# Memory tokens loaded channels first, their weights in packed blocks, and the opening of a four-branch encoder kernel put in another order

## The chip, the cores and the metric

The kernel runs on one NeuronCore of a Trainium2 chip. The metric is the device time of one execution in microseconds, 968.35 us at the median of three runs of the kernel before. The engines are named as the profile names them: PE (TensorE, matmuls), PEld (its weight loads), DVE (VectorE), ACT (ScalarE), POOL (GpSimd), SP (SyncE, which issues most DMAs). Each engine works through its own queue in order and waits on semaphores.

## What is computed

One layer of an encoder, batch 1, 1024 tokens of width 1024, all in float32. Only the parts that the change touches are shown; the four branches of the mixer (`mlstm_chunkwise`, `multiscale_pool`, `rwkv7_time_mix`, `forgetting_attention`) stand between them.

```python
def rms_norm(x, g):
    x32 = x.astype(jnp.float32)
    y = x32 * lax.rsqrt(jnp.mean(x32 * x32, axis=-1, keepdims=True) + NORM_EPS)
    return (y * g).astype(x.dtype)
...
    mem_n = rms_norm(mem, mem_norm_g)             # 256 memory tokens
    h = rms_norm(x, pre_norm_g[l])
    proj = h @ w_in[l] + b_in[l]                  # 1024 x 3728, feeds the four branches
    ...
    x = x + rms_norm(y @ w_out[l], post_norm_g[l])
    hm = rms_norm(x, xattn_pre_g[l])
    # memory attention: k, v = split(mem_n @ wkv), o = softmax(q k / 16) v, o @ wo
    x = x + rms_norm(memory_cross_attention(hm, mem_n, xattn_wq[l], xattn_wkv[l], xattn_wo[l]), xattn_post_g[l])
```

## The kernel before

All products are split in two halves, as `a = hi + lo`: `mm3` (lines 136 to 139) issues three matmuls (hi·hi, hi·lo, lo·hi) into one PSUM group. The hi half is a copy in a rounded type made by ACT, the lo half a subtraction.

The program opens with the **memory stage**, the part that changes. In the order of PE:

1. 16 transposes (line 215) of the two 128 x 1024 tiles of `mem` give `mT` (channels in the partitions), which ACT (line 163) and DVE (line 164) split while they multiply by `mem_norm_g`.
2. Eight blocks `cp` (the loop behind line 259) make `mem @ wkv`, 256 columns each: 8 channel groups x 2 column halves x 3 matmuls of 256 columns, 48 matmuls. The result is multiplied by the memory tokens' inverse norms `RS` (line 268). Blocks 0 to 3 are K and go to DRAM (`kTd`, line 270), 4 to 7 are V and stay as `KV`.
3. In between, after block `cp`, the 128-token tile `cp - 1` of `x` is transposed (`xtile`, line 252: 8 transposes of 128 x 128, in two PSUM tiles of four) and split (lines 160, 161) into `h` and `l`. `xnorm` (lines 240 to 245) has loaded and normalised it: Square with a row sum on ACT (149), a power on POOL (143, 144), and one DVE instruction that multiplies by the inverse norm and by `pre_norm_g` (151). Tiles 6 and 7 are both transposed behind block 7.
4. `vwrow` (line 325 on) multiplies V by `xattn_wo`, four heads of 24 matmuls with 512 columns, copied by ACT (335) and stored to `vwd` (336).

Then the input projection `h @ w_in` starts, and with it the rest of the program (lines 345 on), which the change does not touch.

Weights come in **pieces** of 128 x 512 floats (256 KB) through `wload` (lines 110 to 127): SP issues the load into one of four `wr` buffers (two of `wp1`, two of `wp0`), ACT casts to `wh` (line 122), and the lo half `wl` is made on DVE (line 124) for every second piece and on POOL (line 126) for the others, while `wp0` is open:

```python
            SC.copy(hi, raw)
            if cur["wp0"] is not None and wcount["wr"] % 2:
                V.tensor_tensor(lo, raw, f32(hi), op=ALU.subtract)
            else:
                G.tensor_tensor(lo, raw, f32(hi), op=ALU.subtract)
```

A block of step 2 takes four pieces, and a head of step 4 takes four. A `wr` buffer is free again when its lo half is made; `wh` and `wl` have eight buffers each, free when PE is done with them. A scheduler orders each engine's queue by priority, weight loads ahead of other work; the built program's order is shown below where the change moves it.

Of the kernel before, what the change touches and what calls it, by code (L numbers as in the profile page):

```python
# [36 lines left out]
def tile_trunk(ctx: ExitStack, tc: tile.TileContext, a, out, dbg=None):  # L37
# [143 lines left out]
    xp = Pool("xp", {"x": 2, "xn": 3, "gbc": 1})  # L181
# [20 lines left out]
    V.memset(mhalf, -0.5)  # L202


    mss = m0.one("mss", [128, 2])
    mTh = [m0("mT", [128, 4, 256], F32R) for _ in range(2)]
    mTl = [m0("mT", [128, 4, 256], F32R) for _ in range(2)]
    for kp in range(4):
        if kp == 1:
            tc.cur_priority = pr0  # L210
        p = ps("tr", [128, 2, 256])
        for i in range(2):
            for kk in range(2):
                k = 2 * kp + kk
                T.transpose(p[:, kk, i * 128:(i + 1) * 128], mx_[i][:, k * 128:(k + 1) * 128], ident)
        for kk in range(2):
            q, r = divmod(2 * kp + kk, 4)
            split_evac(mTh[q][:, r, :], mTl[q][:, r, :], p[:, kk, :], mg[:, 2 * kp + kk:2 * kp + kk + 1])
    for i in range(2):
        SC.activation(xp("xn", [128, 1024]), mx_[i], AF.Square, accum_out=mss[:, i:i + 1])  # L220
    mr = rstd_pow("tn", mss, D, EPS, 2)
    rE = m0.one("rE", [128, 2, 128])
    V.tensor_copy(rE, mr[:, :, None].to_broadcast([128, 2, 128]))
    p = ps("tr", [128, 256])
    for i in range(2):
        T.transpose(p[:, i * 128:(i + 1) * 128], rE[:, i, :], ident)
# [13 lines left out]
    def xnorm(i):  # L240
        x_t = xp("x", [128, 1024])
        SY.dma_start(x_t, a["x"][0, i * 128:(i + 1) * 128, :])
        xn = xp("xn", [128, 1024])
        norm_rows(x_t, pg, xn)
        return xn

    def xtile(i, xn):
        ts = slice(i % 4 * 128, (i % 4 + 1) * 128)
        for q in range(2):
            p = ps("tr", [128, 4, 128])  # L250
            for k in range(4):
                T.transpose(p[:, k, :], xn[:, (4 * q + k) * 128:(4 * q + k + 1) * 128], ident)
            w = 2 * (i // 4) + q
            split_evac(hTh[w][:, :, ts], hTl[w][:, :, ts], p)
# [1257 lines left out]
    for g in range(1, 3):  # L1512
# [9 lines left out]
_INS = ["x", "mem", "pre_norm_g", "post_norm_g", "w_in", "b_in", "norm_a_g", "decay_w2", "iclr_a2", "gn_c_g", "gn_c_b",  # L1522
        "w_out", "xattn_post_g", "xattn_wq", "xattn_wkv", "xattn_wo", "cols", "poolbd"]


def _pack(a):

# [13 lines left out]
    return {"cols": np.concatenate([np.eye(128, dtype=cols.dtype), cols], axis=1), "poolbd": pw}  # L1541
# [19 lines left out]
```

## Time and profile before

| | us |
|---|---|
| three runs | 964.66, 968.35, 969.06 |
| the profiled execution, its own time | 968.87 |
| its span, first to last instruction | 967.0 |
| PE busy | 911.7 (94% of the span) |
| DVE, ACT, POOL busy | 577.0, 419.6, 264.3 |

The mean granted TensorE clock is 0.975 of full speed. In rows of the trace a line `start, us, engine line op out<-in xcount [idle before <-releaser]` is one group of equal instructions; PE's times overlap, since matmuls are pipelined, so the distance from one start to the next is what one costs. `x48` counts instructions. A bracket at the end tells how long the engine had stood idle and what ended that.

### The profile page before, as it was taken

The page shows a single profiled execution, that of the slowest core. Times are in us where ns is not written, and L with a number is a line of the kernel's source. Part 1 is how long each engine was busy: PE and PEld are TensorE (multiplying, and loading weights), DVE is VectorE, ACT ScalarE, POOL GpSimd, SP SyncE. Part 2 cuts the span into 40 slices and gives each one's busy share as a digit, 9 for nine tenths or more (in the row PEclk, how much of TensorE's full clock was granted, in tenths as well). Part 3 has the DMA queues.
Part 4 walks back from the last instruction along what each step waited for, and adds up shares of the span by engine and source line. Part 5 has one row for each costly group of instructions (what it writes and reads, how often), then busy time and mean ns, then how long its engine had stood idle before and what let it go on. Part 6 is the DMA issues. An engine that isn't in the chain of part 4 may idle for free. (4 is left out here: it accounts for less than half of the span.)

```text
span 967.0 us, 16286 instructions
## 1 busy us (share of the span) xinstructions
PE 911.7 (94%) x6057; PEld 769.8 (80%) x6057; DVE 577.0 (60%) x1290; ACT 419.6 (43%) x974; POOL 264.3 (27%) x270
## 2 busy tenths in 40 slices
PE   6989999797998999999898988999999999999997
PEld 6987887596777887777676766788887888889997
DVE  6873136887698135796378747566666546654226
ACT  6667255231055334654345135445455434443321
POOL 4654223552121224344333452000000000121211
PEclk9999999887999999999999999999999999999999
DMA  7877411102323512332476466634327211125104
GB/s 237 264 229 256 120 46 35 41 12 71 66 85 117 129 29 72 100 104 88 129 155 174 150 213 226 204 102 134 112 77 260 78 33 45 45 93 180 44 2 174
DMA packets 98255, 114.37 MB, mean 118 GB/s; under 512 B 20929, under 2 KB 76801, under 8 KB 98177
## 3 DMA queue, kind: packets, MB, share of 16 engines
q1 hardware_dynamic: 98176, 113.34, 38.3%
q8 instruction: 48, 0.79, 0.4%
q14 instruction: 31, 0.25, 0.1%
HBM read 84.44 MB, written 28.87 MB: 117 GB/s over the span
## 5 line engine op out<-in xcount | busy, mean ns | idle before, releaser
L126 POOL TENSOR_TENSOR wl<-wr,wh 128x512 fp32r<-128x512 f32 (+2 forms) x98 | 140.4, 1435 | 395.4 <-ACT wh L122 380.3
L137 PE MATMUL mm<-h,wh 128*128 128x512 f32 x528 | 221.5, 419 | 3.0 <-DVE zu L754 2.7
L138 PE MATMUL mm<-l,wh 128*128 128x512 f32 x528 | 210.9, 399 | 0.0
L139 PE MATMUL mm<-h,wl 128*128 128x512 f32 x528 | 210.8, 399 | 0.0
L137 PEld LDWEIGHTS mm<-h,wh 128*128 128x128 f32 x528 | 101.0, 191 | 27.7 <-DVE zu L754 3.1
L139 PEld LDWEIGHTS mm<-h,wl 128*128 128x128 f32 x528 | 101.2, 192 | 23.4
L122 ACT CAST wh<-wr 128x512 fp32r<-128x512 f32 (+2 forms) x122 | 74.7, 621 | 100.9 <-PE mm L138 35.4
L138 PEld LDWEIGHTS mm<-l,wh 128*128 128x128 f32 x528 | 101.3, 192 | 17.7 <-issue 0.5
L137 PE MATMUL mm<-wh,act 128*128 128x256 f32 x256 | 71.8, 281 | 0.0
L138 PE MATMUL mm<-wl,act 128*128 128x256 f32 x256 | 71.0, 277 | 0.0
L139 PE MATMUL mm<-wh,act 128*128 128x256 f32 x256 | 70.8, 277 | 0.0
L137 PE MATMUL mm<-h,act 128*128 128x512 f32 x128 | 53.6, 419 | 0.7 <-ACT jk L1305 0.7
L138 PE MATMUL mm<-l,act 128*128 128x512 f32 x128 | 50.4, 394 | 0.0
L139 PE MATMUL mm<-h,act 128*128 128x512 f32 x128 | 50.4, 394 | 0.0
L137 PEld LDWEIGHTS mm<-wh,act 128*128 128x128 f32 x256 | 48.2, 188 | 0.1
L138 PEld LDWEIGHTS mm<-wl,act 128*128 128x128 f32 x256 | 48.1, 188 | 0.0
L139 PEld LDWEIGHTS mm<-wh,act 128*128 128x128 f32 x256 | 48.0, 188 | 0.0
L137 PE MATMUL mm<-wh,h 128*128 128x260 f32 (+1 forms) x128 | 39.4, 308 | 1.5 <-DVE zu L819 1.5
L137 PE MATMUL mm<-mT,wh 128*128 128x256 f32 x128 | 37.5, 293 | 1.4 <-ACT wh L122 1.4
L139 PE MATMUL mm<-mT,wl 128*128 128x256 f32 x128 | 37.1, 290 | 1.6 <-DVE wl L124 1.6
L138 PE MATMUL mm<-wl,h 128*128 128x260 f32 (+1 forms) x128 | 38.3, 299 | 0.0
L139 PE MATMUL mm<-wh,l 128*128 128x260 f32 (+1 forms) x128 | 38.1, 298 | 0.0
(405 smaller groups left out, 2003.5 us busy)
## 6 DMA issues: line engine op xcount, KB each, us to landing
wr<-in_w_in_dram SPq DMA_DIRECT2D x50, 256.0 KB, 2.9
wr<-in_xattn_wkv_dram SPq DMA_DIRECT2D x32, 256.0 KB, 3.8
x<-in_x_dram SPq DMA_DIRECT2D x16, 512.0 KB, 5.0
x<-x1d SPq DMA_DIRECT2D x15, 512.0 KB, 5.6
wr<-in_xattn_wo_dram SPq DMA_DIRECT2D x16, 256.0 KB, 3.1
vwd<-row SPq DMA_DIRECT2D x8, 512.0 KB, 4.0
rT<-zu SPq DMA_DIRECT2D x16, 256.0 KB, 2.3
zT<-zu SPq DMA_DIRECT2D x16, 256.0 KB, 3.2
```

Source lines behind the costliest of these rows:

```text
L122: SC.copy(hi, raw)
L126: G.tensor_tensor(lo, raw, f32(hi), op=ALU.subtract)
L137: T.matmul(o, lh, rh, start=st, stop=False, skip_group_check=skip)
L138: T.matmul(o, lh, rl, start=False, stop=False, skip_group_check=skip)
L139: T.matmul(o, ll, rh, start=False, stop=sp, skip_group_check=skip)
```

## The change

- `mem` arrives from the host transposed and in partition order (`memT`, 128 x 8 x 256), in four loads of 256 KB; its 16 transposes on PE go. ACT and DVE split it straight from SBUF.
- `xattn_wkv` arrives in packed blocks (`wkv`, 128 x 8 x 8 x 256): a partition's part of a piece is one run of 2 KB where it was two of 1 KB.
- The constants `cst` are loaded through ACT's queue, behind a table load; before, SP issued them first. They now hold `pre_norm_g` as columns, and its broadcast load of 512 KB goes.
- While `wp0` is open, all lo halves of the weight pieces are made on DVE.
- The norms of the memory tokens come from squares in the transposed layout, two sums on DVE, and one float32 matmul with ones (line 225 of the changed kernel), which stands on PE behind block 0; then Ln and Exp on ACT.
- `x` is scaled by its inverse norm alone (a `tensor_scalar`), and `pre_norm_g` is multiplied in when the transposes are split (lines 163, 164).
- `x` is transposed by halves: `xhalf` takes one channel group of four token tiles into one PSUM tile. Tokens 0 to 511 are transposed in two groups of 16, behind blocks 4 and 5, tokens 512 to 1023 in two groups of 16, behind heads 0 and 1 of `vwrow`.

```diff
@@ wload
-            if cur["wp0"] is not None and wcount["wr"] % 2:
+            if cur["wp0"] is not None:
                 V.tensor_tensor(lo, raw, f32(hi), op=ALU.subtract)
@@ the opening
-    xp = Pool("xp", {"x": 2, "xn": 3, "gbc": 1})
+    xp = Pool("xp", {"x": 2, "xn": 6})
...
-    SY.dma_start(cst, a["cols"])
-    mx_ = []
-    for i in range(2):
-        x_t = xp("x", [128, 1024])
-        SY.dma_start(x_t, a["mem"][0, i * 128:(i + 1) * 128, :])
+    tc.keep_in_program_order(SC.preload_act_table_set("natural_log_exp_and_others"))
+    mraw = [xp("xn", [128, 4, 256]) for _ in range(2)]
+    for q in range(4):
+        SY.dma_start(mraw[q // 2][:, q % 2 * 2:q % 2 * 2 + 2, :], a["memT"][:, 2 * q:2 * q + 2, :])
+        if q == 0:
+            SC.dma_start(cst, a["cols"])
+        for k in (2 * q, 2 * q + 1):
+            split_evac(mTh[k // 4][:, k % 4, :], mTl[k // 4][:, k % 4, :], mraw[k // 4][:, k % 4, :], mg[:, k:k + 1])
+        wk0.append(wload(wv[:, 0, 2 * q:2 * q + 2, :]))
...
-    for kp in range(4):
-        p = ps("tr", [128, 2, 256])
-        ...
-                T.transpose(p[:, kk, i * 128:(i + 1) * 128], mx_[i][:, k * 128:(k + 1) * 128], ident)
...
+    def memnorm():
+        for q in range(2):
+            SC.activation(mraw[q], mraw[q], AF.Square)
+        V.tensor_tensor(mraw[0], mraw[0], mraw[1], op=ALU.add)
+        V.tensor_tensor(mraw[0][:, 0:2], mraw[0][:, 0:2], mraw[0][:, 2:4], op=ALU.add)
+        V.tensor_tensor(mraw[0][:, 0], mraw[0][:, 0], mraw[0][:, 1], op=ALU.add)
+        p = ps("tr", [128, 256])
+        T.matmul(p, onesa, mraw[0][:, 0], start=True, stop=True)
+        SC.activation(RS[:, 1, :], p, AF.Ln, bias=eps_n, scale=1.0 / D)
+        SC.activation(RS[:, 1, :], RS[:, 1, :], AF.Exp, scale=-0.5)
+        SC.activation(RS[:, 0, :], RS[:, 1, :], AF.Copy, scale=1.0 / 16)
@@ xnorm and xtile, now xnorm and xhalf
-        norm_rows(x_t, pg, xn)
+        SC.activation(xn, x_t, AF.Square, accum_out=r)
+        r = rstd_pow("tn", r, D, EPS)
+        V.tensor_scalar(xn, x_t, r, None, op0=ALU.mult)
+    def xhalf(hf, k0, nk):
+        for k in range(k0, k0 + nk):
+            p = ps("tr", [128, 4, 128])
+            for i in range(4):
+                T.transpose(p[:, i, :], xn_[4 * hf + i][:, k * 128:(k + 1) * 128], ident)
+            w = 2 * hf + k // 4
+            split_evac(hTh[w][:, k % 4, :], hTl[w][:, k % 4, :], p.rearrange("p a b -> p (a b)"), pg[:, k:k + 1])
@@ the loop over cp
+        if cp == 0:
+            memnorm()
...
-        if cp < 7:
-            xn_[cp + 1] = xnorm(cp + 1)
-        if cp > 0:
-            xtile(cp - 1, xn_[cp - 1])
-    xtile(7, xn_[7])
+        xnorm(cp)
+        if cp in (4, 5):
+            xhalf(0, 4 * cp - 16, 4)
@@ the loop over heads
         vwrow(h, w)
+        if h < 2:
+            xhalf(1, 4 * h, 4)
```

Behind the memory stage each engine's order is that of the kernel before. Three places show what moved within it.

The head of ACT's queue, before (`x_3` is a memory tile, `xn_13` only takes the squares, `wr` and `wh` are pieces of block 0):

```order
L220 ACT_TABLE_LOAD
L220 ACTIVATE xn_13_149,mss_108<-x_3_98 128x1024
L163 ACTIVATE mT_5_109<-tr_9_113,cst_96 128x256
L163 ACTIVATE mT_5_109<-tr_10_122,cst_96 128x256
L220 ACTIVATE xn_14_151,mss_108<-x_4_100 128x1024
L163 ACTIVATE mT_5_109<-tr_9_113,cst_96 128x256
L122 CAST wh_36_190<-wr_35_188 128x512
```

and now (`xn_3`, `xn_4` hold the transposed memory tokens):

```order
L187 ACT_TABLE_LOAD
L198 DMA cst_97<-in_cols_dram 128x214
L163 ACTIVATE mT_5_100<-xn_3_98,cst_97 128x256 x4
L163 ACTIVATE mT_6_101<-xn_4_99,cst_97 128x256 x4
L122 CAST wh_10_112<-wr_9_110 128x512
L220 ACTIVATE xn_3_98<-xn_3_98 128x1024
L122 CAST wh_13_123<-wr_12_121 128x512
```

The first cast of a weight piece stands behind all eight splits of the memory tokens now, and behind the load of `cst`, not behind PE's transposes.

DVE's queue from the end of block 0's pieces to block 1's, now (`xn_37` is token tile 0 of `x`):

```order
L124 TENSOR_TENSOR wl_20_146<-wr_18_143,wh_19_145 128x512
L221 TENSOR_TENSOR xn_3_98<-xn_3_98,xn_4_99 128x1024
L222 TENSOR_TENSOR xn_3_98<-xn_3_98 128x512
L245 TENSOR_SCALAR xn_37_234<-x_36_232,tn_39_237 128x1024
L223 TENSOR_TENSOR xn_3_98<-xn_3_98 128x256
L124 TENSOR_TENSOR wl_43_245<-wr_41_242,wh_42_244 128x512
L124 TENSOR_TENSOR wl_46_263<-wr_44_260,wh_45_262 128x512
L124 TENSOR_TENSOR wl_49_281<-wr_47_278,wh_48_280 128x512
L124 TENSOR_TENSOR wl_52_299<-wr_50_296,wh_51_298 128x512
```

Before, two of a block's four lo halves stood on POOL instead (here those of the last two pieces of block 0 and two of block 1):

```order
L143 TENSOR_SCALAR tn_15_153<-mss_108 128x2
L144 TENSOR_TENSOR tn_15_153<-tn_15_153,mhalf_106 128x2
L126 TENSOR_TENSOR wl_40_209<-wr_38_206,wh_39_208 128x512
L126 TENSOR_TENSOR wl_46_245<-wr_44_242,wh_45_244 128x512
L143 TENSOR_SCALAR tn_33_183<-tn_32_181 128x1
L144 TENSOR_TENSOR tn_33_183<-tn_33_183,mhalf_106 128x1
L126 TENSOR_TENSOR wl_58_294<-wr_56_291,wh_57_293 128x512
```

All four lo halves of a block now stand in a row on DVE behind the scaling of one tile of `x`, which waits for POOL's power; POOL keeps only the powers.

PE between the last block and the first head, before (`xn_748` and `xn_848` are tiles 6 and 7 of `x`):

```order
L139 MATMUL mm_869<-mT_110,wl_927 128x256
L252 MATMUL tr_946<-cst,xn_748 128x128 x4
L252 MATMUL tr_953<-cst,xn_748 128x128 x4
L252 MATMUL tr_960<-cst,xn_848 128x128 x4
L252 MATMUL tr_967<-cst,xn_848 128x128 x4
L137 MATMUL mm_1057<-wh_1010,KV_174 128x512
```

and between the first head and the second, now (the first of four channel groups, and the seam to head 1):

```order
L139 MATMUL mm_1005<-wh_950,KV_168 128x512
L253 MATMUL tr_1014<-cst,xn_575 128x128
L253 MATMUL tr_1014<-cst,xn_689 128x128
L253 MATMUL tr_1014<-cst,xn_803 128x128
L253 MATMUL tr_1014<-cst,xn_889 128x128
```

Two more groups of 16 stand behind blocks 4 and 5 and one behind head 1; between block 7 and head 0 no transposes are left.

## Rows read from the trace of the kernel before

**Rows 1.** Busy time of PE by stretch (from:to in us, length, busy time and count, granted clock, share of the DMA engines, GB/s). The stretches are cut at starts of PE's blocks: the start of the program, blocks 0 and 1, the transposes of tile 0, blocks 2 to 7, the last 16 transposes, the beginning and the rest of `vwrow`, the input projection.

```profile
5.74:10.80 5.06, 3.65 (x17) 1.00 0.98 325
12.14:26.20 14.06, 13.55 (x97) 1.00 0.69 212
26.99:34.06 7.07, 6.03 (x51) 1.00 0.77 253
34.85:40.70 5.85, 5.85 (x52) 1.00 0.97 314
41.49:47.17 5.68, 5.68 (x52) 1.00 0.73 234
47.96:53.79 5.83, 5.83 (x51) 1.00 0.91 305
54.58:60.30 5.72, 5.72 (x51) 1.00 0.86 283
66.93:72.73 5.80, 2.45 (x18) 0.90 0.56 181
72.73:75.02 2.29, 2.29 (x8) 0.50 0.46 138
75.02:96.42 21.40, 21.40 (x92) 1.00 0.82 269
96.42:156.00 59.58, 59.58 (x260) 1.00 0.27 78
```

**Rows 2.** The timeline at the start, engine by engine (start us, us, engine line op, idle before).

```profile
0.72 1.28 ACT L220 ACT_TABLE_LOAD   x1 [0.72 <-PEq L1549]
0.72 0.39 SPq L188 DMA_DIRECT2D cst<-in_cols_dram  x1
1.17 0.89 SPq L193 DMA_DIRECT2D x<-in_mem_dram  x2
2.80 0.20 DVE L295 COPY pc<-cst 128x70 f32<-128x70 f32 x1 [1.14 <-DMA cst<-in_cols_dram]
5.63 1.06 ACT L220 ACTIVATE xn<-x 128x1024 f32<-128x1024 f32 x1 [3.63 <-DMA x<-in_mem_dram]
7.93 0.90 ACT L163 ACTIVATE mT<-tr,cst 128x256 fp32r<-128x256 f32 x2 [1.15 <-PE tr L215]
10.80 0.58 PE L137 MATMUL mm<-mT,wh 128*128 128x256 f32 x1 [1.41 <-ACT wh L122]
13.21 0.58 PE L139 MATMUL mm<-mT,wl 128*128 128x256 f32 x1 [0.51 <-DVE wl L124]
```

**Rows 3.** PE's timeline in block 0, from its first matmuls in close order to the change of pace, and the transposes of tile 0 with the matmul that follows.

```profile
13.60 0.42 PE L137 MATMUL mm<-mT,wh 128*128 128x256 f32 x1
13.81 0.41 PE L138 MATMUL mm<-mT,wh 128*128 128x256 f32 x1
17.01 0.29 PE L138 MATMUL mm<-mT,wh 128*128 128x256 f32 x1
17.13 0.28 PE L139 MATMUL mm<-mT,wl 128*128 128x256 f32 x1
...
26.20 1.03 PE L252 MATMUL tr<-cst,xn 128*128 128x128 f32 x8
26.99 0.36 PE L137 MATMUL mm<-mT,wh 128*128 128x256 f32 x1
```

**Rows 4.** PE's timeline at the last 16 transposes and the first matmuls of `vwrow`.

```profile
66.93 1.03 PE L252 MATMUL tr<-cst,xn 128*128 128x128 f32 x8
70.59 0.66 PE L252 MATMUL tr<-cst,xn 128*128 128x128 f32 x4 [2.63 <-DVE l L161]
71.97 1.11 PE L252 MATMUL tr<-cst,xn 128*128 128x128 f32 x4 [0.72 <-DVE l L161]
74.59 0.60 PE L138 MATMUL mm<-wl,KV 128*128 128x512 f32 x1
75.02 0.41 PE L139 MATMUL mm<-wh,KV 128*128 128x512 f32 x1
75.27 0.39 PE L137 MATMUL mm<-wh,KV 128*128 128x512 f32 x1
```

**Rows 5.** The weight pieces' way, first 100 us: what the SP queue waited for (us in total, times, longest), DMA issues (count, KB each, median us to landing), and the casts and lo halves (count, busy us, mean ns, idle before).

```profile
SPq L115 <- POOL wl L126: 29.9, 21, 3.6
SPq L115 <- DVE wl L124: 13.2, 9, 3.7
...
wr<-in_xattn_wkv_dram SPq DMA_DIRECT2D x32, 256.0 KB, 3.8
x<-in_x_dram SPq DMA_DIRECT2D x8, 512.0 KB, 5.1
wr<-in_xattn_wo_dram SPq DMA_DIRECT2D x16, 256.0 KB, 3.1
...
L126 POOL TENSOR_TENSOR wl<-wr,wh 128x512 fp32r<-128x512 f32 x28 | 43.4, 1556 | 28.4 <-ACT wh L122 24.2 <-DVE wl L124 2.5 <-PE mm L139 1.3
L122 ACT CAST wh<-wr 128x512 fp32r<-128x512 f32 x52 | 31.4, 623 | 15.8 <-DMA wr<-in_xattn_wkv_dram 10.3 <-DMA wr<-in_w_in_dram 2.2 <-DMA wr<-in_xattn_wo_dram 1.8
L124 DVE TENSOR_TENSOR wl<-wr,wh 128x512 fp32r<-128x512 f32 x24 | 28.3, 1184 | 8.2 <-ACT wh L122 8.0
```

**Rows 6.** Durations of other forms (count, busy us, mean ns).

```profile
L161 DVE TENSOR_TENSOR l<-tr,h 128x512 fp32r<-128x512 f32 x25 | 16.7, 683 | 6.0 <-ACT h L160 6.0
L151 DVE SCALAR_TENSOR_TENSOR xn<-x,tn,gbc 128x1024 f32<-128x1024 f32 x8 | 11.3, 1413 | 7.1 <-POOL tn L144 6.3 <-ACT wh L122 0.7
L532 DVE TENSOR_SCALAR gc<-gc 128x512 f32<-128x512 f32 x4 | 1.7, 427 | 3.9 <-ACT gc L525 3.8
L149 ACT ACTIVATE xn<-x 128x1024 f32<-128x1024 f32 x8 | 8.5, 1061 | 4.4 <-DMA x<-in_x_dram 4.4
L144 POOL TENSOR_TENSOR tn<-tn,mhalf 128x1 f32<-128x1 f32 x8 | 4.4, 550 | 0.7
```

**Rows 7.** Stretches in which the granted clock was at the lower of its two levels (columns as in Rows 1).

```profile
71.62:75.02 3.40, 3.05 (x10) 0.50 0.47 152
174.02:180.85 6.83, 6.83 (x20) 0.50 0.13 37
221.81:232.05 10.24, 9.17 (x52) 0.50 0.12 34
```

More of the change, by code (lines that the diff above doesn't have):

```diff
@@ L186, in tile_trunk @@
     tc.cur_priority = -1000
-    cst = base.one("cst", [128, 206])
-    SY.dma_start(cst, a["cols"])
-    ident, mg = cst[:, 0:128], cst[:, 198:206]
-    mx_ = []
-    for i in range(2):
-        x_t = xp("x", [128, 1024])
-        SY.dma_start(x_t, a["mem"][0, i * 128:(i + 1) * 128, :])
-        mx_.append(x_t)
+    tc.keep_in_program_order(SC.preload_act_table_set("natural_log_exp_and_others"))
+    cst = base.one("cst", [128, 214])
+    ident, mg, pg = cst[:, 0:128], cst[:, 198:206], cst[:, 206:214]
+    mraw = [xp("xn", [128, 4, 256]) for _ in range(2)]
+    wv = a["wkv"]
+    wk0 = []
+    mTh = [m0("mT", [128, 4, 256], F32R) for _ in range(2)]
+    mTl = [m0("mT", [128, 4, 256], F32R) for _ in range(2)]
+    for q in range(4):
[5 more added lines that the diff above has]
+        wk0.append(wload(wv[:, 0, 2 * q:2 * q + 2, :]))
     jp = m0.one("jp", [128, 128], mybir.dt.int32)
@@ L202, in tile_trunk @@
     V.memset(mhalf, -0.5)
-    mss = m0.one("mss", [128, 2])
-    mTh = [m0("mT", [128, 4, 256], F32R) for _ in range(2)]
-    mTl = [m0("mT", [128, 4, 256], F32R) for _ in range(2)]
-    for kp in range(4):
-        if kp == 1:
-            tc.cur_priority = pr0
-        p = ps("tr", [128, 2, 256])
-        for i in range(2):
-            for kk in range(2):
-                k = 2 * kp + kk
-                T.transpose(p[:, kk, i * 128:(i + 1) * 128], mx_[i][:, k * 128:(k + 1) * 128], ident)
[L216 to L226, printed above, removed]
-    RS = m0.one("RS", [128, 2, 256])
-    SC.activation(RS[:, 0, :], p, AF.Copy, scale=1.0 / 16)
-    SC.copy(RS[:, 1, :], p)
-    pg = gload(xp, "gbc", a["pre_norm_g"][0])
+    onesa = m0.one("onesa", [128, 128])
+    V.memset(onesa, 1.0)
+    tc.cur_priority = pr0
+    RS = m0.one("RS", [128, 2, 256])
+    def memnorm():
[9 more added lines that the diff above has]
+        SC.activation(RS[:, 0, :], RS[:, 1, :], AF.Copy, scale=1.0 / 16)
     hTh = [hT("h", [128, 4, 512], F32R) for _ in range(4)]
@@ L243, in xnorm @@
         xn = xp("xn", [128, 1024])
-        norm_rows(x_t, pg, xn)
[L245 to L249, printed above, removed]
+        r = base("tn", [128, 1])
+        SC.activation(xn, x_t, AF.Square, accum_out=r)
+        r = rstd_pow("tn", r, D, EPS)
+        V.tensor_scalar(xn, x_t, r, None, op0=ALU.mult)
+        xn_.append(xn)
+    def xhalf(hf, k0, nk):
+        for k in range(k0, k0 + nk):
             p = ps("tr", [128, 4, 128])
[L251 to L254, printed above, removed]
+            for i in range(4):
+                T.transpose(p[:, i, :], xn_[4 * hf + i][:, k * 128:(k + 1) * 128], ident)
+            w = 2 * hf + k // 4
+            split_evac(hTh[w][:, k % 4, :], hTl[w][:, k % 4, :], p.rearrange("p a b -> p (a b)"), pg[:, k:k + 1])
     Vh = [m0("KV", [128, 4, 256], F32R) for _ in range(2)]
     Vl = [m0("KV", [128, 4, 256], F32R) for _ in range(2)]
-    xn_ = {}
-    xn_[0] = xnorm(0)
+    xn_ = []
     for cp in range(8):
         p = ps("mm", [128, 2, 256])
-        for k, wh, wl in wpiece(a["xattn_wkv"][0], cp * 256, 256, 2):
+        for k in range(8):
+            if k % 2 == 0:
+                wp = wk0[k // 2] if cp == 0 else wload(wv[:, cp, k:k + 2, :])
+            wh, wl = (w_[:, k % 2, :] for w_ in wp)
             for c in range(2):
@@ L1520, in tile_trunk @@
     base.close()
-_INS = ["x", "mem", "pre_norm_g", "post_norm_g", "w_in", "b_in", "norm_a_g", "decay_w2", "iclr_a2", "gn_c_g", "gn_c_b",
-        "w_out", "xattn_post_g", "xattn_wq", "xattn_wkv", "xattn_wo", "cols", "poolbd"]
+_INS = ["x", "memT", "post_norm_g", "w_in", "b_in", "norm_a_g", "decay_w2", "iclr_a2", "gn_c_g", "gn_c_b",
+        "w_out", "xattn_post_g", "xattn_wq", "wkv", "xattn_wo", "cols", "poolbd"]
 def _pack(a):
@@ L1540, in _pack @@
         pw[r0:r0 + 64, g // 2, r0:r0 + 64] = w[g]
-    return {"cols": np.concatenate([np.eye(128, dtype=cols.dtype), cols], axis=1), "poolbd": pw}
+    mt = np.asarray(a["mem"][0]).T.reshape(8, 128, 256).transpose(1, 0, 2)
+    wkv = np.asarray(a["xattn_wkv"][0]).reshape(8, 128, 8, 256).transpose(1, 2, 0, 3)
+    return {"cols": np.concatenate([np.eye(128, dtype=cols.dtype), cols], axis=1), "poolbd": pw, "memT": mt, "wkv": wkv}
 def kernel(**inputs):
```

2 lines of the change are left out of this document (1 added, 1 removed).

## The prediction

> **What bounds the kernel now.** I read the busy time of PE by stretch first, since PE does every product [rows 1]. The input projection, from 96.42 on, has PE busy for all of its 59.58 us, and behind it the changed program issues the same instructions in the same order. So the question is when PE starts that projection. In the 96.42 us ahead of it PE loses time in four places, and the reader should see them in this order. First, the opening: PE does its first product at 10.80 and products in close order only from about 13.2, when DVE delivers the first lo half [rows 2]; until 17.0 they follow each other every 0.21 us, behind that every 0.12 [rows 3]. Second, small waits in blocks 0 to 2: block 2 lasts 7.07 us where blocks 3 to 7 last 5.68 to 5.85 without a gap [rows 1]. Third, the last 16 transposes: 5.80 us for 2.45 us of work, with waits of 2.63 and 0.72 us for DVE's split of earlier transposes [rows 4]. Fourth, the clock: within those transposes the granted clock falls to the lower level (1.2 of 2.4 GHz), from 71.62 to 75.02 [rows 7], and the first products of `vwrow` run in it.
>
> A block without a wait is at the same time close to what loads allow: blocks 3 and 5 move 314 and 305 GB/s with 0.97 and 0.91 of the DMA engines busy [rows 1].
>
> The sum is made against the profiled execution's own 968.87 us, 0.52 above the median of the three runs. A difference of 0.5% is 4.8 us, about what a measurement of this kernel can tell from no change.
>
> **The change part by part.**
>
> *1. The start: -3.0.* Removed are 16 transposes, the wait for 1 MB of tokens in row form, and two passes of squares that stood ahead of the splits on ACT [rows 2]. The first 256 KB piece of `memT` should land where the 512 KB load did, at 5.63, or somewhat sooner. `cst` now leaves ACT behind the table load, which ends at 2.00; it took 2.1 us from issue to landing (0.72 to 2.80), so about 4.5 to 5 with other loads beside it. ACT then makes eight hi halves at about 0.43 each (two took 0.90 up to the next instruction, less the gap; [rows 2]), from 5 to 8.5, and the first cast of 0.62 [rows 5]: first product about 9.1. DVE makes eight lo halves of 256 columns at the same 0.43 to 0.48, with the fourth piece of tokens in by 6.5, and the first lo half of a weight piece at 0.68 [rows 6]: close order from about 10.2 instead of 13.2. The bounds: 8.9 (`cst` as quick as before) and 12.2 (`cst` 2 us later: nothing in the trace shows ACT's queue issuing a load behind a table load with others in flight). I take 10.2, nearest to the one row that times this load. The 3.4 us at the slow pace I leave in its place, moved ahead as a whole.
>
> *2. Blocks 0 to 4, waits that go: -1.35; waits that come: +1.5 (0 to +4).* The loader's ring held each piece for its load (3.8), cast (0.62) and lo half; SP waited 29.9 us for POOL's lo halves and 13.2 for DVE's [rows 5]. POOL takes 1.56 for one, DVE 1.18 [rows 5], while the same form (128x512, subtract) takes DVE 0.683 in `split_evac` [rows 6]; a DVE that doesn't share with POOL is the likeliest reading. So four lo halves in a row cost 2.8 on DVE instead of 1.18 on it beside 1.56 on POOL, and all 48 cost 33 us instead of 28.3 for 24. With a piece ready in 3.8 + 0.62 + 0.69 = 5.1 instead of 6.0, block 2 should fall from 7.07 to the 5.72 of block 6: -1.35. Against it stands what now queues ahead of the four lo halves: Square (1.06), POOL's powers (0.55 [rows 6] and a smaller operation), the scaling of 1024 columns (0.427 for 512 [rows 6], so 0.7 to 0.85), then 2.76 for the lo halves: 5.2 to 5.7 in a row, against a block every 5.7 us on PE where it was every 6.5, since no transposes stand behind blocks 1 to 3 any more (8 took 0.79, [rows 3]). And the loads of such a block, 1 MB of weights, 0.5 of `x` and what comes early of the rest, need 5.7 us at the 314 GB/s of block 3. So the 0.79 us taken out behind each of four blocks partly turn into waits for pieces; they come back as transposes behind blocks 4 and 5 while the waits stay. Of 4 x 0.8 = 3.2 some half is hidden by the lead of the loads: +1.5. Nil if the loader runs ahead; +4 if each block waits a full microsecond.
>
> *3. The last transposes: -4.2.* They move between heads 0 and 1 and 1 and 2. Their waits came from `tr` buffers that DVE had not yet split. A group is now 16 transposes into exactly four PSUM tiles that the previous group, a block or a head earlier, has long left. So 16 x 0.099 = 1.58 (eight took 0.79, [rows 3]) stand in place of 5.80. The split behind them, 4 x 0.683 on DVE, lies beside a head of some 5 us; tokens 512 to 1023 are first read by the input projection's second half.
>
> *4. The clock behind them: -1.2.* Without those waits it has no cause here to fall: the six products from 72.73 that ran at 0.43 instead of 0.23 us [rows 4] gain 0.195 each.
>
> A page speaks against terms 3 and 4. What the rows show: six times eight transposes stood between two blocks (0.79 us, [rows 3]), and the blocks behind them ran at a granted clock of 1.00 [rows 1]; it fell only where waits of 3.4 us stood among 16 [rows 4]. The Trainium skill, page "TensorE: Matmul & The Clock Gate", section "Part 4: PE-mode transpose", says that transpose-mode instructions do not count as PE activity in the way products do, and that the full clock does not engage for them. By that rule the four groups of 16, 1.6 us each, could each cost a fall of the clock; the rows have no group of that length without a wait, so it is a rival below.
>
> *5. The float32 product with ones: +0.5.* One product of 128x256 in plain float32 behind block 0; the trace has no such form. Below: a product at 0.12 [rows 3]; above: four of them and one drain, 0.85. It also waits if the squares and three sums are late, which stand behind block 0's last lo half. I take the middle.
>
> *Costed at nothing.* The `gbc` load of 512 KB goes: it lay in the loads' shadow behind block 0; without that cover it would be 1.6 us in our favour at 314 GB/s. The `xn` pass on DVE, 1.413, falls to about 0.8; hidden, already counted in term 2. Multiplying by `pre_norm_g` at the split adds about 0.1 to each of 16 instructions on DVE and ACT; it lies beside products, and exposed would be under 1. On SP each tile's load of `x` stands one block earlier, ahead of weight pieces that it delays by up to 512 KB, 1.6 us; the ring's lead covers it, and if not it is inside the +4 above. ACT's splits behind blocks 4 and 5 wait for those blocks' end, with the next casts queued behind them; those pieces have a block's time, 5.7 us, of cover, and uncovered each group would cost PE about 2. Token tiles 6 and 7 wait for a free `xn`, until the group behind block 4 is done; they have two blocks' time.
>
> Sum: -3.0 - 1.35 + 1.5 - 4.2 - 1.2 + 0.5 = -7.75. From 968.87 this is 961.1, forecast **961**; the input projection then starts near 88.7. From the median it would be 960.6.
>
> **The rivals.** *A: the loader keeps its old pace.* If lo halves don't fall to 0.69 on DVE alone, or `x` loads stand in the pieces' way, four blocks still come every 6.5 us (4 x 0.79 = 3.2 in place of 1.5) and block 2's 1.35 stays: 3.0 above the sum, 964.1; with the late start of term 1 (+2) 966. For it: loads at 0.97 in block 3. Against it: SP's 43 us of waits were for lo halves, not for loads [rows 5].
>
> *B: the transposes lower the clock for a short time.* Each of four groups is followed by 3.4 us at the lower level, as after the last transposes now [rows 7], 1.7 lost each: +6.8, 967.9, no change. For it: the one group of 16 was followed by a fall. Against it: the fall began within waits [rows 4, 7].
>
> *C: slower.* The same, but each fall lasts as long as the one at 174.02, 6.83 us, or at 221.81, 10.24 [rows 7]: lost 3.4 each, +13.7, 974.8. It decides from an average fall of 6 us on (12 us lost over four groups is 973). Those falls followed stretches in which PE waited; a group between two full blocks has none. It could also come of this: a group waits for a token tile whose scaling is late, and the wait with the transposes drops the clock.
>
> *D: the start doesn't move*, because `cst` behind the table load is late by more than the 3 us: 964.1, no change.
>
> **How the numbers follow.** Forecast with its own spread (bounds of terms 1, 2 and 5) 0.68; A 0.14; B 0.08; C 0.04; D 0.06. The forecast's own ends are -1.3 to +2 (term 1), -1.5 to +2.5 (term 2) and ±0.4; not all at one end at once, so 957.5 to 965. The range 957 to 966 holds it, A and D. Faster by over 0.5% is below 964.0 from the profiled time, 963.5 from the median: nearly all of the forecast, and a third of A, 0.72. Slower by over 0.5% is above 973.2: C. The rest, 0.24, is the same.
>
> **What would show it.** First product near 9 and close order near 10; no lo halves on POOL in the opening and DVE's at 0.69 mean; SP's waits for lo halves well below 43 us; groups of 16 transposes in 1.6 us behind blocks 4 and 5 and heads 0 and 1, with the granted clock at 1.00 behind each; the input projection at 88.7. I am wrong if that start is at 92 or later, if blocks 1 to 4 come every 6 us or more, or if the clock falls between 40 and 80 us.

## The result, and the profile after

The changed kernel took 962.5 us, the median of 19 runs, against 967.48 for the kernel before, also 19 runs: a ratio of 0.995, interval 0.9933 to 0.9967, or 4.8 us gained (3.2 to 6.5). The forecast was 961, the range 957 to 966. One of the changed kernel's 19 runs, 1007.87 us at a mean granted clock of 0.839, is left out of the ratio. The profiled execution took 964.69 (span 962.8), 4.2 less than that of before.

The sum, though, was made for one moment, the start of the input projection, and there the gain is 8.1 us. The timeline of PE in the changed kernel at that start (start us, us, engine line op), which was 96.42 before [rows 1]:

```profile
88.08 0.39 PE L139 MATMUL mm<-wh,KV 128*128 128x512 f32 x1
88.31 0.39 PE L137 MATMUL mm<-h,wh 128*128 128x512 f32 x1
```

So there are two questions: did the 8.1 us come from where the sum said, and where did some 3 of them go?

The stretches of the opening in the changed kernel (from:to, length, then busy time and count of PE, PEld, DVE, ACT and POOL, granted clock, share of the DMA engines, GB/s): blocks 1 to 4, the first group of transposes, block 5, the second group, blocks 6 and 7, head 0, the third group, head 1, the fourth, heads 2 and 3.

```profile
17.82:23.50 5.68, 5.68 (x48) 5.65 (x47) 3.86 (x7) 4.01 (x8) 0.74 (x2) 1.00 0.98 339
23.50:29.30 5.80, 5.80 (x52) 5.80 (x51) 3.60 (x7) 3.33 (x7) 0.74 (x2) 1.00 0.92 288
29.30:35.00 5.70, 5.70 (x50) 5.70 (x49) 3.63 (x7) 3.42 (x6) 0.74 (x2) 1.00 0.93 289
35.00:40.78 5.78, 5.78 (x52) 5.78 (x51) 3.18 (x6) 3.77 (x7) 0.74 (x2) 1.00 0.89 293
40.78:42.44 1.66, 1.66 (x18) 1.66 (x17) 1.66 (x4) 0.79 (x2) 0.00 (x0) 1.00 1.00 354
42.44:48.28 5.84, 5.84 (x52) 5.84 (x51) 5.71 (x10) 4.35 (x8) 0.00 (x0) 1.00 0.91 305
48.28:51.04 2.76, 1.88 (x18) 1.64 (x17) 1.76 (x3) 1.72 (x3) 0.00 (x0) 1.00 0.84 289
51.04:56.70 5.66, 5.66 (x51) 5.66 (x50) 5.52 (x9) 5.49 (x11) 0.00 (x0) 1.00 0.62 201
56.70:62.48 5.78, 5.78 (x50) 5.78 (x49) 5.78 (x11) 4.97 (x11) 2.62 (x4) 1.00 0.57 181
62.48:68.03 5.55, 5.55 (x26) 4.46 (x25) 4.66 (x8) 4.29 (x8) 0.00 (x0) 1.00 0.74 241
68.03:69.69 1.66, 1.66 (x17) 1.66 (x16) 1.28 (x3) 1.52 (x4) 0.00 (x0) 1.00 1.03 311
69.69:75.40 5.71, 5.71 (x27) 4.57 (x26) 4.44 (x7) 4.85 (x9) 0.00 (x0) 1.00 0.91 321
75.40:77.06 1.66, 1.66 (x17) 1.66 (x16) 0.33 (x2) 1.33 (x3) 0.00 (x0) 1.00 0.76 219
77.06:88.31 11.25, 11.25 (x51) 9.12 (x50) 4.38 (x8) 8.10 (x16) 3.84 (x3) 1.00 0.66 214
```

In every stretch but one PE's busy time fills the length: PE waits only in the second group of transposes, 0.88 us. The granted clock is 1.00 in all of them.

The start, in the timeline of the changed kernel:

```profile
0.72 1.28 ACT L187 ACT_TABLE_LOAD   x1 [0.72 <-PEq L1557]
0.75 0.39 ACTq L198 DMA_DIRECT2D cst<-in_cols_dram  x1
4.77 0.20 DVE L298 COPY pc<-cst 128x70 f32<-128x70 f32 x1 [2.97 <-DMA cst<-in_cols_dram]
4.83 3.30 ACT L163 ACTIVATE mT<-xn,cst 128x256 fp32r<-128x256 f32 x8 [2.83 <-DMA cst<-in_cols_dram]
8.69 0.58 PE L137 MATMUL mm<-mT,wh 128*128 128x256 f32 x1 [8.69 <-ACT wh L122]
9.56 0.58 PE L139 MATMUL mm<-mT,wl 128*128 128x256 f32 x1
```

ACT issues `cst` at 0.75, while its table load (0.72 to 2.00) still runs; the first reader starts at 4.77, about 2 us later than before [rows 2]. The eight splits on ACT wait for it, then take 3.30 us; products come in close order from 9.56, where they came from 13.21.

The lo halves of the first 97 us by engine (columns as in Rows 5):

```profile
L124 DVE TENSOR_TENSOR wl<-wr,wh 128x512 fp32r<-128x512 f32 x48 | 31.5, 686 | 5.2 <-ACT wh L122 5.0
L126 POOL TENSOR_TENSOR wl<-wr,wh 128x512 fp32r<-128x512 f32 x5 | 6.4, 1293 | 27.4 <-ACT wh L122 27.4
```

DVE's lo half fell from 1184 ns to 686. The five on POOL belong to the input projection's first pieces. SP's waits for them in the first 100 us:

```profile
SPq L115 <- DVE wl L124: 32.3, 45, 2.0
...
SPq L115 <- POOL wl L126: 6.9, 4, 2.7
```

In all 39.2 us, hardly less than before.

Behind 88.31 the lead shrinks in two ways. Between that start and the transposes of the last stage (line 1448 before, 1453 now) it goes from 8.11 to 7.23; the clock falls at other places in the two executions there, in all 44.4 us at the lower level before and 41.0 now, so the sum of the falls does not explain it. In the last stage itself the lead goes from 7.23 to 4.35, with 0.3 us of waits of PE in either kernel and at a granted clock of 1.00. The first row of that stage on PE, the first product that reads `act`, and the last row, before:

```profile
781.53 0.38 PE L1448 MATMUL tr<-cst,e 128*128 128x128 f32 x2
864.97 0.28 PE L137 MATMUL mm<-wh,act 128*128 128x256 f32 x1
960.36 0.28 PE L139 MATMUL mm<-wh,act 128*128 128x256 f32 x1
```

and in the changed kernel:

```profile
774.30 0.38 PE L1453 MATMUL tr<-cst,e 128*128 128x128 f32 x2
857.72 0.28 PE L137 MATMUL mm<-wh,act 128*128 128x256 f32 x1
956.01 0.28 PE L139 MATMUL mm<-wh,act 128*128 128x256 f32 x1
```

That is 178.83 us before and 181.71 now for the same instructions. Up to the first product with `act` (the attention weights that `vwd` is multiplied by) it is 83.4 us in both; all of the difference lies behind it, 95.39 and 98.29. In the last 60 us the products follow each other every 113.3 ns before and every 118.3 now (mean of the distances between starts in the trace, over the whole 60 us).

### The profile page after: what moved, and what is told of

Same layout as the page of the kernel before. It is cut to its first block, busy times and chain, and to the rows that moved or that the text cites. A ratio compares the mean times of both kernels' runs of the same rounds, so it can differ in the third digit from the quotient of the medians.

```text
span 962.8 us, 16248 instructions
## 1 busy us (share of the span) xinstructions
PE 908.3 (94%) x6041; PEld 768.9 (80%) x6041; DVE 577.4 (60%) x1317; ACT 421.1 (44%) x973; POOL 227.8 (24%) x244
## 5 line engine op out<-in xcount | busy, mean ns | idle before, releaser
L126 POOL TENSOR_TENSOR wl<-wr,wh 128x512 fp32r<-128x512 f32 (+2 forms) x74 | 101.5, 1372 | 392.3 <-ACT wh L122 377.5
L1499 DVE TENSOR_TENSOR o<-mm,gb 128x256 f32<-128x256 f32 x32 | 13.6, 424 | 43.8 <-ACT junk L1498 43.5
```

The lines of the kernel that those rows point to most:

```text
L1499: V.tensor_tensor(o3[i][:, gs], p, xog[:, gs], op=ALU.mult)
```

## The experiments

Twelve runs were made, in three groups, each group on one chip together with the kernel before: again, narrow, wide and tile; dveonly, pool, pad and best; best5, unpacked, before2 and dveonly2. "Input projection" is its start in the profile; "last stage" is the time between the first and the last of the three rows shown above; the interval of a ratio is in brackets.

| run | ratio to before | first product | input projection | last stage |
|---|---|---|---|---|
| before (first profile) | | 10.80 | 96.42 | 178.83 |
| before2 | one run | 11.08 | 97.27 | 178.62 |
| changed (first profile) | 0.995 [0.9933, 0.9967] | 8.69 | 88.31 | 181.71 |
| again | 0.9927 [0.990, 0.9954] | 8.59 | 87.29 | 181.80 |
| narrow | 0.9914 [0.9884, 0.9944] | 8.95 | 87.83 | 178.83 |
| wide | 1.0023 [1.0002, 1.0045] | 10.02 | 95.48 | 181.80 |
| tile | 0.9928 [0.9899, 0.9956] | 8.75 | 87.63 | 181.70 |
| dveonly | 0.9975 [0.9959, 0.9992] | 10.40 | 94.64 | 181.26 |
| dveonly2 | one run | 10.50 | 94.44 | 178.80 |
| pool | 0.9981 [0.9961, 1.000] | 8.59 | 91.10 | 181.80 |
| pad | 0.9943 [0.9924, 0.9961] | 8.65 | 87.60 | 182.82 |
| unpacked | 0.9934 [0.9913, 0.9954] | 8.86 | 88.00 | 181.69 |
| best | 0.9963 [0.9945, 0.9981] | 6.34 | 93.07 | 181.30 |
| best5 | 0.9956 [0.994, 0.9971] | 6.49 | 94.93 | 178.80 |

### Where the lead goes: again, narrow, wide, pad

**again** is the changed kernel without an edit.

> The changed kernel once more, nothing edited. In its first profile the input projection began at 88.31 us, 8.1 earlier than before, but the program ended only 4.2 earlier, and the medians of 19 runs differ by 5.0. Both theories: the opening repeats, input projection at 88.3 within 0.3. Theory L (the constants tile is 32 bytes per partition wider, which moves every later tile of SBUF): from there to the end it takes 874.5 within 1 again, and the products of the last 60 us follow each other every 118 ns where they did every 113 before. Theory C (the clock's falls land elsewhere in each execution, and the last pace is chance): from there to the end anything from 868 to 876, the last pace 113 or 118. Ratio to the kernel before 0.995.

The opening repeats within 1.0 us, the last stage within 0.1 and its pace to the tenth (118.3). The start of the input projection, 87.29, lies outside the 0.3 expected by both theories. From there to the end it took 871.4 us where the first profile took 874.5 and theory L allowed 1 us: the part between the input projection and the last stage varies by some 3 us between executions, the last stage does not.

**narrow** gives `pre_norm_g` a small tile of its own:

```diff
-    cst = base.one("cst", [128, 214])
+    cst = base.one("cst", [128, 206])
-    ident, mg, pg = cst[:, 0:128], cst[:, 198:206], cst[:, 206:214]
+    ident, mg = cst[:, 0:128], cst[:, 198:206]
+    pg = m0.one("pg", [128, 8])
-            SC.dma_start(cst, a["cols"])
+            SC.dma_start(cst, a["cols"][:, 0:206])
...
+        if cp == 1:
+            SY.dma_start(pg, a["cols"][:, 206:214])
```

> The changed kernel with the constants tile 206 columns wide as before, pre_norm_g in a small tile of its own in a pool that is closed ahead of the input projection, so that every tile behind that stands where it stood in the kernel before. Theory L: input projection at 88.3, last pace 113 ns, 870.5 us from the input projection to the end, ratio 0.9917 (8 us gained). Theory C: the same ratio as the changed kernel, 0.995, and either pace.

The timeline of its last stage on PE:

```profile
770.29 0.38 PE L1456 MATMUL tr<-cst,e 128*128 128x128 f32 x2
949.12 0.28 PE L139 MATMUL mm<-wh,act 128*128 128x256 f32 x1
```

178.83 again, pace 113.3. Its ratio is the lowest of all, 0.9914; the interval overlaps that of the changed kernel, and its median is 1.3 us under that of again, so between these two the 3 us show in the traces and not in the times.

**wide** does the reverse to the kernel before, and touches nothing else:

```diff
-    cst = base.one("cst", [128, 206])
+    cst = base.one("cst", [128, 214])[:, 0:206]
```

> The kernel before with its constants tile allotted 214 columns, of which 206 are loaded and used as before; nothing else. Theory L: input projection at 96.4, last pace 118 ns, some 873 to 874.5 us from there to the end where it was 870.5, ratio 1.003 to 1.004. Theory C: ratio 1.000 within 0.0015, either pace.

```profile
776.78 0.38 PE L1448 MATMUL tr<-cst,e 128*128 128x128 f32 x2
958.58 0.28 PE L139 MATMUL mm<-wh,act 128*128 128x256 f32 x1
```

181.80 us, pace 118.3: the kernel before gets the last stage of the changed one by 32 bytes per partition that nobody uses. Its ratio, 1.0023, is 2.2 us (0.2 to 4.4). From the input projection to the end, though, this profile took 869.7 us where theory L wanted 873 to 874.5: the part ahead of the last stage was 3.8 us shorter than in the first profile of the kernel before (681.30 against 685.11) and covers the stage's 3.0.

**pad** widens the tile of the changed kernel by 32 bytes more:

```diff
-    cst = base.one("cst", [128, 214])
+    cst = base.one("cst", [128, 222])[:, 0:214]
```

> The changed kernel with its constants tile allotted 222 columns (64 bytes per partition more than before, 32 more than in the changed kernel), 214 of them used. In six profiles so far the last 60 us had products every 113.3 ns where the tile has 206 columns and every 118.3 where it has 214. If that hangs on the position of later tiles modulo 64 bytes: 113.3 again, ratio like that of the narrow tile, 0.9915 to 0.993. If any shift does it: 118.3.

Neither of the two: 120.0 ns and 182.82 us.

```profile
772.26 0.38 PE L1453 MATMUL tr<-cst,e 128*128 128x128 f32 x2
955.08 0.28 PE L139 MATMUL mm<-wh,act 128*128 128x256 f32 x1
```

So it is no matter of a step of 64 bytes. Over all profiles: six with 214 columns took 181.69 to 181.80, in five different programs; one with 222 took 182.82; five with 206 took 178.62 to 178.83. Two with 206 (dveonly, best) took 181.26 and 181.30, at 117.8 ns. These two are of pad's group, in which 214 columns (pool) took 181.80: there the step from 206 to 214 is 0.5 us, and that to 222 another 1.0. To place these, both programs of dveonly and before ran again side by side.

**before2** and **dveonly2** are those programs unedited.

> The kernel before once more. Input projection at 95.5 to 96.5. If the last pace belongs to the program, products of the last 60 us every 113.3 ns as in its first profile; if it belongs to the execution or the chip, 117.8 here, the other value seen with a constants tile of 206 columns.

> The kernel of the run dveonly once more, on the same chip as before2. If the last pace belongs to the program: 117.8 again, with 113.3 in before2. If to the chip: both alike. If to the execution: any.

Both show 113.3 (178.62 and 178.80; before2 started its input projection at 97.27, 0.8 later than expected), so 117.8 in dveonly was not the program's. Whether the chip or the execution made it is open. What stands is that a wider constants tile, alone, adds 2.9 to 3.2 us to the last stage where 206 columns run at 113.3 ns (the changed kernel and wide against before and before2, narrow against again), and that 206 columns can have an execution that is nearly as slow. That the widening moves later tiles to other places is the likely reason, since wide changes nothing else; which tile's place does it was not tried.

### Where the lead comes from: tile, dveonly, pool, unpacked

**tile** puts the transposes of `x` back to their places, eight per token tile, the last 16 ahead of the heads. The multiplication by `pre_norm_g` is left out.

```diff
-        if cp in (4, 5):
-            xhalf(0, 4 * cp - 16, 4)
+        if cp > 0:
+            xtile(cp - 1)
...
+    xtile(7)
     w = vwprep(0)
...
-        if h < 2:
-            xhalf(1, 4 * h, 4)
```

> The changed kernel with the transposes of x put back: eight per token tile behind blocks 1 to 7 and the last eight ahead of the heads. It leaves out the multiplication by pre_norm_g. My account of the opening (transposes 10.54 us before, 7.74 now; low clock behind the last ones 1.2): input projection at 88.3 + 2.8 + 1.2 = 92.3, a wait of 2 to 4 us among the last 16 and a fall of the granted clock there, time 4 us above the changed kernel (ratio 0.999). If the blocks were dense only because no transposes stood between them, the blocks also come every 6.5 us again and the input projection starts at 92.5 to 93.5.

This falsifies my account of the transposes. Input projection at 87.63, between the two profiles of the changed kernel, where I expected 92.3. The last 16 transposes of this run:

```profile
62.64:64.30 1.66, 1.66 (x18) 1.66 (x17) 1.66 (x4) 1.01 (x2) 0.00 (x0) 1.00 0.59 180
```

The last 16 take 1.66 us in the very place where they took 5.80 before [rows 4], without a wait and without a fall of the clock.

**dveonly** is the kernel before with one edit, the lo halves:

```diff
-            if cur["wp0"] is not None and wcount["wr"] % 2:
+            if cur["wp0"] is not None:
```

> The kernel before with one edit: all lo halves of weight pieces on DVE while the first weight pool is open. Theory S (DVE and POOL slow each other; DVE's late splits made the waits among the last 16 transposes and between the blocks, not the place of the transposes): DVE's lo halves fall from 1.18 to 0.69 us, blocks 1 to 7 come without a wait, the last 16 transposes take 1.7 instead of 5.8 us, no fall of the clock there; first product at 10.8 as before, input projection at about 90 (96.4 less 1.4 of waits, 4.1 of transposes, 1.2 of clock), ratio 0.9935. Theory P (the place of the transposes): the last 16 still take over 4 us, input projection at 94 to 96, ratio 0.998 or more.

The input projection at 94.64 is where theory P put it, and the ratio, 0.9975, is just below P's 0.998, but not for P's reason, which wanted the last 16 transposes at over 4 us. The scheduler answered the edit with one more shift: the transposes of tile 0 come in two groups of four, in block 0 and behind block 1. This program has two profiles. Block 7, the last 16 transposes and `vwrow` in dveonly:

```profile
59.89:66.54 6.65, 6.10 (x51) 5.89 (x50) 5.19 (x9) 4.29 (x8) 0.75 (x2) 1.00 0.49 152
66.54:68.66 2.12, 2.05 (x19) 1.63 (x17) 2.12 (x4) 1.43 (x3) 0.00 (x0) 1.00 0.92 316
68.66:94.64 25.98, 22.96 (x99) 17.98 (x98) 12.79 (x22) 18.21 (x34) 3.83 (x3) 1.00 0.76 249
```

and in dveonly2:

```profile
59.24:65.07 5.83, 5.83 (x51) 5.83 (x50) 5.07 (x8) 3.78 (x9) 0.74 (x2) 1.00 0.50 152
65.07:66.74 1.67, 1.67 (x19) 1.67 (x17) 1.67 (x4) 1.64 (x3) 0.00 (x0) 1.00 0.88 261
66.74:94.44 27.70, 24.55 (x100) 19.12 (x98) 12.58 (x22) 18.87 (x36) 4.71 (x4) 0.94 0.75 257
```

The last 16 transposes took 2.12 and 1.67 us with no fall of the clock, where their order was that of before: nearly all of that loss was the engine of the lo halves, as theory S has it. The kernel before shows the delay in its rows of POOL and DVE:

```profile
64.83 3.96 POOL L126 TENSOR_TENSOR wl<-wr,wh 128x512 fp32r<-128x512 f32 x2 [0.19 <-ACT wh L122]
65.88 3.46 DVE L124 TENSOR_TENSOR wl<-wr,wh 128x512 fp32r<-128x512 f32 x2
69.86 0.68 DVE L161 TENSOR_TENSOR l<-tr,h 128x512 fp32r<-128x512 f32 x1
71.83 0.68 DVE L124 TENSOR_TENSOR wl<-wr,wh 128x512 fp32r<-128x512 f32 x1
```

Two lo halves on DVE took 3.46 us beside two on POOL, and the split that PE waited for (at 70.59, [rows 4]) came behind them; a lo half on DVE while POOL stood idle took 0.68.

What S missed is what came late next. Blocks 5 to 7 took 6.25, 6.44 and 6.65 us in dveonly, some 2 us more than dense blocks, but 5.83, 5.72 and 5.83 in dveonly2: that loss is the execution's. In both the lead went in `vwrow`, which took 25.98 and 27.70 us where it took 23.69 before. PE waited there for ACT's copies of its results (line 335) alone, in dveonly and in dveonly2:

```profile
PE mm L137 <- ACT row L335: 3.0, 2, 1.7
PE mm L137 <- ACT row L335: 3.2, 2, 2.0
```

In dveonly2 the clock also fell behind the second of these waits, from 85.39 to 88.81. Why ACT comes late there, and which other part of the change prevents it in the changed kernel, was not tried.

**pool** is the counterpart: the changed kernel with every second lo half on POOL again.

```diff
-            if cur["wp0"] is not None:
+            if cur["wp0"] is not None and wcount["wr"] % 2:
```

> The changed kernel with every second lo half on POOL again, as before the change; the rest of the change stays. Theory S: DVE's and POOL's lo halves take 1.2 and 1.5 us, waits for pieces return in blocks 1 to 4 and in the groups of transposes, input projection at 91 to 93 instead of 87.3 to 88.3, ratio 0.997 to 0.999. Theory P: within 1 us of the changed kernel, input projection at 89 or sooner.

Input projection at 91.10, 2.8 to 3.8 later than in the changed kernel's profiles, just above the start of the expected 91 to 93; ratio 0.9981.

```profile
L126 POOL TENSOR_TENSOR wl<-wr,wh 128x512 fp32r<-128x512 f32 x28 | 39.0, 1401 | 39.9 <-ACT wh L122 37.2 <-DVE wl L124 2.7
L124 DVE TENSOR_TENSOR wl<-wr,wh 128x512 fp32r<-128x512 f32 x24 | 23.1, 966 | 9.5 <-ACT wh L122 9.5
```

With POOL at work DVE's lo half takes 966 ns where it takes 686 alone, and POOL's 1401. The Trainium skill, page "GPSIMD Engine Reference", section "1. Specifications", says that GpSimd shares its SBUF interfaces with VectorE and contends with DVE instructions that have two SBUF inputs. The rows agree on both sides of the rule: DVE's split of the transposes, one of whose inputs is in PSUM, took 683 ns in the kernel before [rows 6], and 0.69 us at 61.70, wholly beside a lo half on POOL from 61.26 to 62.56, while the lo halves, both of whose inputs are in SBUF, took 1184 ns [rows 5].

**unpacked** reads `wkv` from its original layout.

```diff
-    wv = a["wkv"]
+    wv = a["xattn_wkv"][0].rearrange("(k p) (b c) -> p b k c", p=128, c=256)
```

> The changed kernel, but wkv read from its original layout, two runs of 1 KB for each partition and piece; all else stays. My prediction priced the packing at nothing. If that is right: input projection at 87.3 to 88.3 as in the changed kernel. If the packing is what lets the loads keep up with dense blocks (DVE-only lo halves alone left waits of 2 us in blocks 4 to 6): waits for pieces in the blocks, input projection at 89.5 to 91.

Input projection at 88.00, ratio 0.9934: the packing is worth nothing that these runs can tell.

### Two attempts at an earlier start: best, best5

**best** lets the first product wait for a quarter of the memory tokens instead of all; `kp` pins an instruction behind the one written before it on its engine. It has the narrow tile, and the second group behind block 6:

```diff
+    kp = tc.keep_in_program_order
+    kp(SY.dma_start(cst, a["cols"][:, 0:206]))
     for q in range(4):
+        kp(SY.dma_start(mraw[q // 2][:, q % 2 * 2:q % 2 * 2 + 2, :], a["memT"][:, 2 * q:2 * q + 2, :]))
...
+        kp(SY.dma_start(raw, wv[:, 0, 2 * q:2 * q + 2, :]))
         for k in (2 * q, 2 * q + 1):
...
+            kp(SC.activation(h_, m_, AF.Copy, scale=mg[:, k:k + 1]))
+            kp(V.scalar_tensor_tensor(l_, m_, mg[:, k:k + 1], f32(h_), op0=ALU.mult, op1=ALU.subtract))
+        kp(SC.copy(hi, raw))
+        kp(V.tensor_tensor(lo, raw, f32(hi), op=ALU.subtract))
...
-        if cp in (4, 5):
-            xhalf(0, 4 * cp - 16, 4)
+        if cp in (4, 6):
+            xhalf(0, 2 * cp - 8, 4)
```

> The narrow constants tile; constants first on SP; then for each quarter of the memory tokens its load, its weight piece, its two splits and the piece's cast and lo half in this order, so that the first product needs a quarter of the tokens; second group of 16 transposes of x behind block 6 instead of 5. If PE's start hangs on ACT's and DVE's order: first product at 5.5 to 6 instead of 8.7, input projection at 84 to 85, last pace 113.3, ratio 0.987 to 0.989. If loads bound the opening, the lead is lost again in blocks 1 and 2 and the input projection starts at 87, ratio 0.991.

The first product came at 6.34, 2.3 us sooner, and blocks 0 to 4 were done at 37.78 instead of 40.78. Then the first group of transposes waited, since the scheduler had put the load of token tile 3 behind block 6's pieces:

```profile
37.78 1.47 PE L260 MATMUL tr<-cst,xn 128*128 128x128 f32 x12
...
49.15 1.11 PE L260 MATMUL tr<-cst,xn 128*128 128x128 f32 x4 [5.83 <-DVE xn L252]
```

and the stretch at the lower clock that began in this wait:

```profile
48.02:54.85 6.83, 5.70 (x27) 5.70 (x28) 5.02 (x8) 4.14 (x7) 1.03 (x3) 0.50 0.73 244
```

The wait of 5.8 us and the 6.83 us at the lower clock, with 5.70 of work in them, gave back more than the start had gained: the input projection came at 93.07, 4.8 later than in the changed kernel's first profile, though blocks 0 to 4 had been done 3.0 sooner.

**best5** asks for tiles 3 and 4 of `x` earlier and moves the groups behind blocks 5 and 6.

```diff
-        SY.dma_start(x_t, a["x"][0, i * 128:(i + 1) * 128, :])
+        with tc.high_priority() if i in (3, 4) else nullcontext():
+            SY.dma_start(x_t, a["x"][0, i * 128:(i + 1) * 128, :])
...
-        if cp in (4, 6):
-            xhalf(0, 2 * cp - 8, 4)
+        if cp in (5, 6):
+            xhalf(0, 4 * cp - 20, 4)
```

> The kernel of the run best with the loads of x put back among the weight pieces (tiles 3 and 4 of x asked for early) and the groups of transposes behind blocks 5 and 6. In best the first group waited 5.8 us for token tile 3, and the clock fell behind it for 6.8 us, 3.4 lost. Expected: first product at 6.3 again, no wait of over 1 us in a group, no fall of the clock ahead of the heads, input projection at 93.1 - 5.8 - 3.4 = 84, ratio 0.987 to 0.990. If loads bound the blocks, their lead is lost and the input projection starts at 86 to 88.

Wrong again, in another way: the token tiles were there, but the second group waited for DVE's splits of the first, 2.66 and 1.98 us, and the clock fell in it.

```profile
53.84:61.32 7.48, 2.84 (x18) 2.40 (x17) 5.31 (x10) 4.81 (x11) 0.74 (x2) 0.79 0.81 254
58.11:64.93 6.82, 5.20 (x25) 5.23 (x26) 5.26 (x9) 5.53 (x12) 0.74 (x2) 0.50 0.79 265
```

(The second group, and the lower clock that began in it; the first group took 1.66.) Neither version beats the changed kernel; narrow has the lowest ratio.

## Why the prediction was right, and which of its steps were not

The time fell into the range on the side that was forecast, and the start of the input projection came at 88.31 where 88.7 was forecast. Both are nearer than the reasoning deserves. At the input projection two misses cancel: waits of 1.5 us that did not come, and transposes that gained 1.4 less. At the end, 4.8 us were gained where 7.75 were forecast; 961 is close to 962.5 also because the forecast started from 968.87, 1.4 above the median of the kernel before. Point by point:

- **Term 1, the start (-3.0).** Close order came 3.65 us sooner, at 9.56. But block 1 ended only 2.70 sooner (23.50 against 26.20), product with ones included: I had left the slow pace "in its place, moved ahead as a whole", and it did not move as a whole. The slow pace ended at 15.14 instead of 17.01 (in both traces the first record of a granted clock of 1.00 begins there), so the slow products filled 5.6 us instead of 3.8. The time of `cst` was right by luck: I had it issued at 2.00, behind the table load, and 2.5 to 3 us on its way; it was issued at 0.75 and took 4.0.
- **Term 2 (-1.35, +1.5).** The first part came: block 2 lasted 5.80 instead of 7.07. The second did not: blocks 1 to 7 are dense, though DVE has the scaling and four lo halves in a row. What I had as a sign of it was no sign: SP's waits for lo halves fell only from 43.1 us [rows 5] to 39.2, and PE waits in none of these blocks.
- **Term 3, the transposes (-4.2).** The groups measured 1.66, 2.76, 1.66 and 1.66, in all 7.74; before, six tiles of 0.79 and the last 16 of 5.80, in all 10.54. So -2.8: a transpose takes 104 ns there and not 99, and one group waits 0.88 for DVE. The four PSUM tiles had not been left long before: DVE split the last of the first group at 49.83, behind lo halves, when the second group already stood waiting. The main reason was wrong too: "they move" explains nothing, as the run tile shows. The waits came from DVE's lo halves, slowed by POOL, ahead of the splits (dveonly and dveonly2: 2.12 and 1.67 us for the last 16 in the old order).
- **Term 4, the clock (-1.2).** `vwrow` without its groups took 22.51 (25.83 less 3.32) against 23.69: -1.18, with no fall of the clock.
- **Term 5 (+0.5).** 0.24 (17.58 to 17.82), two records for the one product, and no wait.
- **The sum** at the input projection: -2.70 - 1.44 (blocks 2 to 7) - 2.80 - 1.18 = -8.12, forecast -7.75.
- **The step that failed** is the first paragraph's: behind that start the changed program issues the same instructions in the same order, so the lead goes through. The instructions are the same, but they do not take the same time. With the eight columns of `pre_norm_g` in the constants tile the last stage takes 2.9 us more, all of it in the products that read `act`; narrow takes this away and wide brings it to the kernel before, by the width of that tile alone. 8.1 less 2.9 is 5.2, with 4.8 (3.2 to 6.5) measured. The order of ACT's queue showed the wider tile (128x214), and I priced it at nothing without naming it. That it acts by the place of the tiles behind it is argued, not shown.
- **Rival A** did not occur. **B and C** did not occur in this kernel: four groups of 16 without a fall. The mechanism of C, a group that waits and a clock that falls, did occur in best and best5, and cost there more than the earlier start had gained. **D** did not occur: `cst` came 2 us later, and the start still moved.
- **The rule on transposes** (the Trainium skill, "TensorE: Matmul & The Clock Gate", "Part 4: PE-mode transpose"): the trace does not bear out a price for it here. Three groups of 1.66 us and one of 2.76 stood between products with the clock at 1.00 behind each; it fell within groups that waited 5.8 us (best) and 4.6 (best5), and in dveonly2 at 85.39, behind a wait of 2.0 us with no transpose near.

## What to carry to other kernels

Before an edit to one stage is credited with the whole of its gain, look at what it moves for the others: here a few columns more in the constants tile cost a third of the gain (2.9 of 8.1 us) in a stage that the diff does not touch. When PE waits for a split, ask first how long the splitting engine takes with its neighbour at work and without; here the engine of the lo halves mattered and the place of the transposes did not. And a lead gained at the start is only kept if what the next stage waits for keeps up with it: dveonly lost its lead in `vwrow`, best and best5 in their groups of transposes.

## What the runs showed of the hardware that was not expected

- PE's pace for the same products in the last stage, without a wait and at a granted clock of 1.00, was 113.3, 118.3 or 120.0 ns with a constants tile of 206, 214 or 222 columns (824, 856, 888 bytes per partition); which of the tiles behind it matters was not tried. 117.8 was seen twice with 206, in one group of runs; one of these two programs showed 113.3 in another.
- The part between the input projection and the last stage took 679.3 to 686.0 us over 14 profiles, with 31 to 44 us at the lower clock. That is a spread of 6.7 us, nearly as wide as that of the 19 runs of the kernel before (963.31 to 970.76).
- A clock that fell within a wait of 5.8 us among transposes (best) stayed low for 6.83 us although PE was busy for 5.70 of them.
- DVE's lo half took 686 ns with POOL idle and 966 to 1184 on average with POOL making every second one; two that ran beside two of POOL's took 3.46 us together.
